# A transformer layer with a 16384-expert feed-forward: the gathered experts cut to 35 slots per token, their overflow listed per token half, and the last U blocks moved into the pipeline

## The chip, the cores and the metric

The kernel is written in Bass and Tile for one Trainium2 chip and runs on one of its cores. A core has TensorE (PE, matrix products into PSUM), VectorE (DVE), ScalarE (ACT), GpSimd (POOL) and SyncE (SP); each runs its own queue in order, and they wait for each other by semaphores. PE, DVE, ACT and POOL compute; SP and POOL issue DMAs here. The metric is the device time of one execution in microseconds (us). The profile is one execution recorded instruction by instruction.

## The reference, cut to what matters

The layer takes 256 tokens of width 2048 through a retention group and an RG-LRU group, a cross attention, and a feed-forward of 16384 single-neuron experts (PEER), then a final norm. Only the last is touched:

```python
def peer_ffn(xn, w_q, sub_keys, u_tab, v_tab):
    ...
    q = (xt @ w_q).reshape(t, PEER_HEADS, 2, PEER_HALF)
    sub_scores = jnp.einsum('thcd,hckd->thck', q, sub_keys).astype(jnp.float32)
    vals, ids = lax.top_k(sub_scores, PEER_TOPK)
    cand = vals[:, :, 0, :, None] + vals[:, :, 1, None, :]
    top_sc, pos = lax.top_k(cand.reshape(t, PEER_HEADS, PEER_TOPK * PEER_TOPK), PEER_TOPK)
    ...
    eid = (i1 * PEER_N_KEYS + i2).reshape(t, PEER_HEADS * PEER_TOPK)
    gate = jax.nn.softmax(top_sc, axis=-1).reshape(t, PEER_HEADS * PEER_TOPK)
    ...
        u = u_tab[eb]
        act = jax.nn.gelu(jnp.einsum('td,tkd->tk', xb, u).astype(jnp.float32))
        return jnp.einsum('tk,tkd->td', (gb * act).astype(xb.dtype), v_tab[eb])
```

Each token picks 128 experts (8 heads of 16). For each, the dot product of the token with the expert's row of `u_tab` goes through a gelu, is weighted by the gate, and scales the expert's row of `v_tab`, which is added to the token.

## The kernel before

**Two ways for the experts.** The table is cut by a row number, (i1 + i2) mod 128. Rows 0 to 95 (`RD`) are computed for all tokens as dense products: U gives the activations, the gates multiply them (zero where a token did not pick the expert), V gives the sum. Rows 96 to 127 are gathered: for each token the picked experts of these rows are fetched one by one. One gather (`rows`, L1132) brings one expert's row for each of the 128 tokens of a half, a megabyte, with an indirect DMA on POOL's queue. A token half has `BASE` = 36 slots, 72 in both; each slot costs a gather from `Us` with a `dot` (L1149, DVE) and a gather from `Vs` with an `axpy` (L1159, DVE).

**Overflow.** A token with more than 36 such experts puts the rest in two lists of 128 entries (`OV`) that both halves share. `compact` (L778) makes the slots and lists: picks by maxima on DVE, places by small matmuls on PE. `spill` (L1204) later fetches each list's U rows, its tokens' rows from `hn`, and its V rows (six gathers of a megabyte), takes the dots, and writes the weights as a one-hot matrix `oh`; sixteen matmuls (L971 to L974 or L994 to L998) add the V rows to their tokens in V chunk 9. If the lists do not hold everything, `rest` (L1226) runs a slow path under an `If`.

**Dense part.** Experts are in 12 chunks (`NCH`) of 8 blocks of 128. Each fp32 weight tile of 512 KB is loaded on SP, split by ACT (`hi`, a cast) and DVE (`lo`, the remainder), and multiplied in two parts. A U block takes two such tiles (halves) and 16 matmuls each; a V quarter takes one tile and 12.

**Order.** Up to the pipeline a planner orders the work, in the kernel's order as far as data allow: `u_chunk` (L928) does chunks 0 to 5 (`LEAD`), 96 halves. Beside them `Weave` feeds side work: after each half `pump` lets generators run for `wv.rate` credits, and each `yield` costs what it names. `RB` = 1.9 is the rate there. The side work is, in order, the rest of `route` (the top-16 searches, DVE), `gbuild` (L859) and `compact`. `gbuild` makes the dense gates: 64 groups of four tokens, each two comparisons on DVE, four scalings on ACT (L874), four matmuls `G` on PE (L884), and a copy on ACT (L886) into `gs`, which has two buffers; every fourth group one DMA on SP writes 768 KB to `gd` in DRAM. Chunk 5 has a stop: after its third block (L939 to L941) all that is left of `gbuild` is run, then `prep(0)` (L897) loads the gates of chunk 0, multiplies them on and splits the result.

From there `run` (L1079) issues by hand a list of steps, with up to 8 loads ahead: 6 times V chunk i (16 steps) and U chunk i + 6 (16 steps), woven with the `prep_steps` (L1041) of the next chunk; then V chunks 6 to 10 alone (80 steps). In all 272 steps with a weight tile. Within the list each engine's order is the order of the code. After each step `pump` at `RC` = 1.17 runs `chosen` (L1169), which does dots and axpys (2.2 credits each, and 0.225 per slot for the gates of a block, `weigh`, L1142), gathering three tasks ahead into four buffers (`ring`). What is left of it after the list is drained (L1360). Then come `rest` and `v_final` (L1247): V chunk 11, the last sums, the final norm and the output.

Of the kernel before, what the change touches and what calls it, by code (L numbers as in the profile page):

```python
# [32 lines left out]
RA, RB, RC = 1.1, 1.9, 1.17  # L33
# [38 lines left out]
def hybrid_layer_kernel(ctx: ExitStack, tc: tile.TileContext, a: dict, out: bass.AP, dbg=None):  # L72
# [705 lines left out]
    def compact():  # L778
        ct = pgt.tile([P, 7, TT], F32, tag="ct", name="ct")
        cnt, more, off, end, tok, off1, end1 = (ct[:, n] for n in range(7))  # L780
# [23 lines left out]
        V.tensor_scalar(fit, end, float(OV * P), None, op0=ALU.is_le)  # L804
# [14 lines left out]
        spl["t"] = tp.tile([P, OV], F32, tag="spt", name="spt")  # L819
        spl["ti"] = tp.tile([P, OV], I32, tag="spti", name="spti")  # L820
        spl["i"] = tp.tile([P, OV], I32, tag="spi", name="spi")
        spl["g"] = tp.tile([P, 40], F32, tag="spg", name="spg")[:, :OV]
# [633 lines left out]
```

## Time and profile before

| | us |
|---|---|
| three runs: lowest, median, highest | 2092.3, 2092.89, 2096.95 |
| the profiled execution, its own time | 2099.48 |
| its span, first to last instruction | 2097.7 |
| PE, DVE, ACT, POOL busy | 2030.7, 1698.7, 1039.0, 342.0 |
| loads of U tiles, V tiles (192 each), median to landing | 4.9, 7.9 |
| gathers from `Us`, `Vs` into `gat`, median to landing | 9.4, 9.6 |
| mean granted TensorE clock | 0.993 |

Busy time is the union of an engine's instructions. A matmul's end is modelled, so the pace of matmuls (how many in a stretch) says more than their busy time. The windows view gives, for stretches of the span in us, each engine's busy time and number of instructions, then the clock granted to PE, the busy share of the 16 DMA engines and the GB/s that they moved. In the timeline a row is: start, duration, engine, line, operation, output <- input, number, and in brackets the idle time before and what ended it.

### The profile page before, as it was taken

To read this page: it belongs to the slowest core of one execution; us is meant where nothing else is said; L and a number is where in the kernel's file an instruction comes from. 1 tells how busy PE (TensorE), PEld (TensorE's weight loads), DVE (VectorE), ACT (ScalarE), POOL (GpSimd) and SP (SyncE) were. 2 spreads that over 40 slices of the span, in tenths; PEclk is the share of its full clock that TensorE was granted. 3 is DMA by queue.
4 is the path that set the end of the run, shared out by engine and by line. 5 is a ranking of instruction groups with operands and counts; after the bars stand their busy time and mean duration, and the time that the engine had idled before them with its cause. 6 is when DMAs were issued, how large, how long until landed. Compare 5 with 4: busy or idle time off the path is not lost.

```text
span 2097.7 us, 29005 instructions
## 1 busy us (share of the span) xinstructions
PE 2030.7 (97%) x10452; PEld 1721.0 (82%) x10452; DVE 1698.7 (81%) x2455; ACT 1039.0 (50%) x1600; POOL 342.0 (16%) x195
## 2 busy tenths in 40 slices
PE   8999999999999999999999989999999999989997
PEld 6888878888888888888889968888888888767785
DVE  6859866744554457999987779999999999989897
ACT  6565434544544455554578853444444444433334
POOL 0200021000000000000000002323333332445342
PEclk9999999999999999999999999999999999999999
DMA  8675646566654468555686579999999999999874
GB/s 283 236 233 171 218 134 184 172 191 190 184 170 141 143 188 283 170 182 179 192 275 192 171 242 371 389 382 400 362 354 358 351 378 409 375 371 391 315 263 157
DMA packets 155015, 542.92 MB, mean 259 GB/s; under 512 B 17136, under 2 KB 44400, under 8 KB 136560
## 3 DMA queue, kind: packets, MB, share of 16 engines
q1 hardware_dynamic: 132832, 400.48, 56.7%
q0 software_dynamic: 22032, 140.53, 16.9%
q8 instruction: 82, 1.34, 0.3%
q14 instruction: 69, 0.57, 0.1%
HBM read 541.99 MB, written 18.87 MB: 267 GB/s over the span
## 4 chain that ended last, share of the span: by engine, by line
PE 77%; DVE 14%; DMA 4%; issue 3%; ACT 1%; POOL 1%; ACTq 0%; DVEq 0%; SPq 0%; POOLq 0%
PE U L129 13%; PE wb L129 8%; PE U L131 7%; PE xc L171 6%; PE xc L172 6%; PE xc L174 6%; PE acc L956 5%; PE acc L953 5%; PE acc L954 5%; PE wb L131 4%; DVE lo L120 4%; PE G L884 2%; PE V L956 2%; PE V L953 2%; PE V L954 2%
## 5 line engine op out<-in xcount | busy, mean ns | idle before, releaser
L120 DVE TENSOR_TENSOR lo<-raw,hi 128x1024 fp32r<-128x1024 f32 x396 | 486.0, 1230 | 261.9 <-PE xc L174 118.8
L119 ACT CAST hi<-raw 128x1024 fp32r<-128x1024 f32 x396 | 415.3, 1050 | 301.2 <-PE xc L172 165.2
L1092 ACT CAST hi<-raw 128x1024 fp32r<-128x1024 f32 x272 | 283.9, 1049 | 265.6 <-PE acc L954 91.1
L129 PE MATMUL U<-xn,hi 128*128 128x512 f32 x1536 | 401.7, 398 | 7.8 <-ACT hi L119 6.1
L1098 DVE TENSOR_TENSOR lo<-raw,hi 128x1024 fp32r<-128x1024 f32 x272 | 328.2, 1221 | 35.0 <-issue 16.6
L129 PEld LDWEIGHTS U<-xn,hi 128*128 128x128 f32 x1536 | 277.8, 190 | 58.3 <-ACT hi L119 6.2
L1135 POOL DMA_INDIRECT gat<-in_Us_dram,idx x69 | 122.2, 1771 | 682.6 <-DVE gat L1152 424.5
L131 PEld LDWEIGHTS U<-xn,lo 128*128 128x128 f32 x1536 | 210.1, 190 | 18.3 <-DVE lo L120 2.3
L131 PE MATMUL U<-xn,lo 128*128 128x256 f32 x1536 | 218.5, 284 | 1.8 <-DVE lo L120 1.3
L1152 DVE SCALAR_TENSOR_TENSOR gat<-gat,h 128x2048 f32<-128x2048 f32 x69 | 157.7, 2285 | 0.0
L953 PE MATMUL acc<-hi,ah 128*128 128x512 f32 x384 | 150.7, 392 | 1.5 <-DVE foldu L937 1.5
L954 PE MATMUL acc<-hi,al 128*128 128x512 f32 x384 | 150.4, 392 | 0.0
L129 PE MATMUL wb<-hT,hi 128*128 128x512 f32 x448 | 119.8, 400 | 0.0
L956 PE MATMUL acc<-lo,ah 128*128 128x512 f32 x384 | 103.4, 391 | 4.9 <-DVE lo L120 3.4
L1135 POOL DMA_INDIRECT gat<-in_Vs_dram,idx x39 | 86.7, 2223 | 130.3 <-DVE hh L1160 112.7
L129 PE MATMUL wb<-xT,hi 128*128 128x512 f32 x368 | 93.4, 394 | 2.1 <-ACT hi L119 2.1
L129 PEld LDWEIGHTS wb<-hT,hi 128*128 128x128 f32 x448 | 81.3, 189 | 14.0
L1160 DVE SCALAR_TENSOR_TENSOR hh<-gat,coef,hh 128x2048 f32<-128x2048 f32 x39 | 91.5, 2346 | 0.1
L956 PEld LDWEIGHTS acc<-lo,ah 128*128 128x128 f32 x384 | 71.9, 188 | 21.8 <-DVE lo L120 4.7
L1135 POOL DMA_INDIRECT h<-in_Vs_dram,idx x33 | 70.7, 2144 | 108.3 <-DVE hh L1160 101.5
L953 PEld LDWEIGHTS acc<-hi,ah 128*128 128x128 f32 x384 | 72.5, 189 | 16.8 <-DVE foldu L937 1.8
L954 PEld LDWEIGHTS acc<-hi,al 128*128 128x128 f32 x384 | 72.6, 189 | 15.2
(411 smaller groups left out, 3654.4 us busy)
## 6 DMA issues: line engine op xcount, KB each, us to landing
raw<-in_U_dram SPq DMA_DIRECT2D x192, 512.0 KB, 4.9
raw<-in_V_dram SPq DMA_DIRECT2D x192, 512.0 KB, 7.9
raw<-in_w_xyg_dram SPq DMA_DIRECT2D x48, 512.0 KB, 4.5
raw<-in_w_qkv_dram SPq DMA_DIRECT2D x48, 512.0 KB, 4.2
raw<-in_w_xk_dram SPq DMA_DIRECT2D x32, 512.0 KB, 3.6
raw<-in_w_xv_dram SPq DMA_DIRECT2D x32, 512.0 KB, 4.2
raw<-in_w_out_dram SPq DMA_DIRECT2D x32, 512.0 KB, 4.2
raw<-in_w_xq_dram SPq DMA_DIRECT2D x32, 512.0 KB, 3.5
```

Of the source, the lines that this page charges most:

```text
L119: A.copy(hi, raw)
L120: V.tensor_tensor(lo, raw, hi.bitcast(F32), op=ALU.subtract)
L129: PE.matmul(pt, hi[:, ks], xt[:, kb, :], start=(kb == 0), stop=(kb == KB - 1))
L131: PE.matmul(pt[:, :T], lo[:, ks], xt[:, kb, :T], start=False, stop=False)
L171: PE.matmul(pt, xh, hi[:, w], start=(n == 0 and k == 0), stop=False)
L953: PE.matmul(pt, ah[:, c, t_], hi[:, w], start=(first and c == 0), stop=False)
L954: PE.matmul(pt, al[:, c, t_], hi[:, w], start=False, stop=False)
L956: PE.matmul(pt, ah[:, c, t_], lo[:, w], start=False, stop=(last and c == 7))
L1092: A.copy(his[t], raws[t])
L1098: V.tensor_tensor(los[t], raws[t], his[t].bitcast(F32), op=ALU.subtract)
L1135: G.indirect_dma_start(gat, None, a[tab], bass.IndirectOffsetOnAxis(ap=idx[tt][:, k:k + 1], axis=0), bounds_check=NS - 1, oob_is_err=False)
L1152: V.scalar_tensor_tensor(gat, gat, 1.0, h[0], op0=ALU.mult, op1=ALU.mult, accum_out=dots[tt, k0][:, k:k + 1])
```

## The change

Seven edits go together. The slots are 35 per token half (70, from 72). The overflow has one list of 128 for each half, with its own tokens only, so the places need one matmul and each list one matmul per kind of column. `compact` takes turns with `gbuild`, yield by yield, and ends with filling the gather buffers (three zero fills, on POOL; they were on DVE). In `gbuild` every second copy is DVE's, and the write to `gd` is issued on POOL. `RB` is 2.35. Chunk 5 does two blocks (`CUT`) in `u_chunk`; its other six are 12 steps at the head of the list, woven with the `prep_steps` of chunk 0, and the stop for `gbuild` is gone; `hh` is loaded at step 8. `spill` is gone: `chosen` ends with the six gathers, two dots, and the weights, and the list's V rows are added by eight matmuls as the last row operations of V chunk 11, in `v_final`. The warm-up of ACT's square root in `v_final` now reads `oh`.

```diff
-RA, RB, RC = 1.1, 1.9, 1.17
+RA, RB, RC = 1.1, 2.35, 1.17
...
-BASE = 36
+BASE = 35
...
-OV = 2
 LEAD = 6
+CUT = 2
...
     def compact():
...
-        PE.matmul(pt[:, 0:1], tri[:, :P], cnt[:, 0:1], start=True, stop=True)
-        PE.matmul(pt[:, 1:2], ones, cnt[:, 0:1], start=True, stop=False)
-        PE.matmul(pt[:, 1:2], tri[:, :P], cnt[:, 1:2], start=False, stop=True)
+        PE.matmul(pt[:, :TT], tri[:, :P], cnt, start=True, stop=True)
...
-        own = rp.tile([P, TT, OV * P], F32, tag="eq", name="own")
...
-        for tt in range(TT):
-            for b, (first, last) in enumerate(((off, end), (off1, end1))):
-                cut = tp.tile([P, P], F32, tag="gj", name="cut")
-                ts, os = slice(tt, tt + 1), slice(b * P, (b + 1) * P)
-                V.tensor_scalar(own[:, tt, os], iota, first[:, ts], fit[:, ts], op0=ALU.is_ge, op1=ALU.mult)
-                V.tensor_scalar(cut, iota, last[:, ts], fit[:, ts], op0=ALU.is_ge, op1=ALU.mult)
-                V.tensor_tensor(own[:, tt, os], own[:, tt, os], cut, op=ALU.subtract)
+        own = rp.tile([P, TT, P], F32, tag="eq", name="own")
+        yield 0.8
+        for tt in range(TT):
+            cut = tp.tile([P, P], F32, tag="gj", name="cut")
+            ts = slice(tt, tt + 1)
+            V.tensor_scalar(own[:, tt], iota, off[:, ts], fit[:, ts], op0=ALU.is_ge, op1=ALU.mult)
+            V.tensor_scalar(cut, iota, end[:, ts], fit[:, ts], op0=ALU.is_ge, op1=ALU.mult)
+            V.tensor_tensor(own[:, tt], own[:, tt], cut, op=ALU.subtract)
             yield 0.8
...
+        for b in range(TT):
+            bs = slice(b, b + 1)
             pt = sm("spill")
             for n, cols in enumerate((lambda tt: sel[tt][:, BASE:], lambda tt: gsp[tt],
...
-                for tt in range(TT):
-                    PE.matmul(pt[:, c0:c1], own[:, tt, os], cols(tt), start=(tt == 0), stop=(tt == TT - 1))
+                PE.matmul(pt[:, c0:c1], own[:, b], cols(b), start=True, stop=True)
             yield 1.5
...
             yield 0.6
...
-    side = []
+        ring.extend(slot("ms", [P, D], f"gat{n}") for n in range(3))
+        for gat in ring:
+            G.memset(gat, 0.0)
+        ring.append(h[1])
+
+    def turns(one, two):
+        for x in one:
+            yield x
+            y = next(two, None)
+            if y is not None:
+                yield y
+        yield from two
+
+    ring = []
...
                 for j in range(4):
                     PE.matmul(pt[:, j * RD:(j + 1) * RD], o1[:, j, :], o2[:, j, :RD], start=True, stop=True)
                 g0 = 4 * (m % 4)
-                A.copy(gs[:, :, g0:g0 + 4, :],
-                       pt[:, :4 * RD].rearrange("p (t c x) -> p c t x", t=4, x=8))
+                (V.tensor_copy if m % 2 else A.copy)(
+                    gs[:, :, g0:g0 + 4, :], pt[:, :4 * RD].rearrange("p (t c x) -> p c t x", t=4, x=8))
                 if m % 4 == 3:
                     tl = slice(4 * m - 12, 4 * m + 4)
-                    nc.sync.dma_start(gd[:, :, tl, :].rearrange("q p t c -> p q t c"), gs)
+                    G.dma_start(gd[:, :, tl, :].rearrange("q p t c -> p q t c"), gs)
                 yield 0.4
...
-    def prep(i):
...
-    def u_chunk(i):
+    ahs, spare = {}, {}
...
-        for c in range(8):
+        for c in blocks:
...
             for j in range(0 if i or c else 1, 2):
                 whalf(j, a["U"][8 * i + c, j], xn, pt)
-                tick(2 * c + j)
...
             A.activation(act[:, c, :], t, AF.Gelu_apprx_tanh)
-            if i == LEAD - 1 and c == 2:
-                while "gbuild" not in done:
-                    wv.pump(3.0)
-                wave.append(prep(0))
-        flush()
...
-        late = i == SPILL + 2
+        late = i == NCH - 1
...
         if late:
             for tt in range(TT):
-                for b in range(OV):
-                    PE.matmul(pts[tt], spl["oh"][:, b, tt * P:(tt + 1) * P],
-                              spl["v"][b][:, dc * 512:(dc + 1) * 512], start=False, stop=(last and b == OV - 1))
+                PE.matmul(pts[tt], spl["oh"][:, tt], spl["v"][tt][:, dc * 512:(dc + 1) * 512],
+                          start=False, stop=last)
...
-                late = i == SPILL + 2
-                v_mms(ah, al, hi, lo, q, list(enumerate(box)), not kept or i == 0, not kept and not late)
-                if late and q == 3:
-                    for tt in range(TT):
-                        for b in range(OV):
-                            PE.matmul(box[tt], spl["oh"][:, b, tt * P:(tt + 1) * P],
-                                      spl["v"][b][:, dc * 512:(dc + 1) * 512], start=False,
-                                      stop=(not kept and b == OV - 1))
+                v_mms(ah, al, hi, lo, q, list(enumerate(box)), not kept or i == 0, not kept)
 
...
         for t, step in enumerate(steps):
+            if t == 8:
+                for tt in range(TT):
+                    nc.sync.dma_start(hh[tt], hd[tt])
...
-    def chosen(blocks):
...
+        dots_left = sum(t[0] is dot for t in tasks)
+        extra = [lambda: fetch(next_gat(), a["Us"], NS, spl["i"][:, 0:1]),
+                 lambda: spill_x(1, next_gat()),
+                 lambda: fetch(next_gat(), a["Us"], NS, spl["i"][:, 1:2])] if tail else []
         for m in range(len(tasks) + AHEAD):
             if m < len(tasks):
                 f, tab, tt, k0, n, k = tasks[m]
                 held.append(rows(tab, tt, k0 + k))
+            elif extra:
+                held.append(extra.pop(0)())
...
                 if f is dot and not any(t[0] is dot and t[2] == tt for t in tasks[m - AHEAD + 1:]):
                     hold(min([t[2] for t in tasks[m - AHEAD + 1:] if t[0] is dot], default=tt))
+                    if tail and not dots_left:
+                        spill_x(0, h[0])
                 yield 2.2
+        if tail:
+            spill_dot(0, held[-3], h[0])
+            spl["v"] = [next_gat() for b in range(TT)]
+            yield 2.2
+            spill_dot(1, held[-1], held[-2])
+            yield 2.2
+            spill_rows()
+            spill_weights()
...
-    def spill():
-        od = cp.tile([P, OV], F32, name="od")
-        for b in range(OV):
-            bs = slice(b, b + 1)
-            u, x = fetch("Us", spl["i"][:, bs], "ah"), fetch(None, spl["ti"][:, bs], "al")
-            yield
-            yield
-            V.scalar_tensor_tensor(u, u, 1.0, x, op0=ALU.mult, op1=ALU.mult, accum_out=od[:, bs])
-            yield
-        spl["v"] = [fetch("Vs", spl["i"][:, b:b + 1], ("ah", "al")[b]) for b in range(OV)]
+    def fetch(dst, src, n, ix):
+        G.indirect_dma_start(dst, None, src, bass.IndirectOffsetOnAxis(ap=ix, axis=0),
+                             bounds_check=n - 1, oob_is_err=False)
+        return dst
+
+    def next_gat():
+        turn[0] += 1
+        return ring[(turn[0] - 1) % len(ring)]
+
+    def spill_x(b, dst):
+        if b == 0:
+            kept_h[0] = None
+        return fetch(dst, hn, T, spl["ti"][:, b:b + 1])
+
+    def spill_dot(b, u, x):
+        if b == 0:
+            spl["d"] = cp.tile([P, TT], F32, name="od")
+        V.scalar_tensor_tensor(u, u, 1.0, x, op0=ALU.mult, op1=ALU.mult, accum_out=spl["d"][:, b:b + 1])
...
+    def spill_weights():
+        od = spl["d"]
...
+        spl["oh"] = rp.tile([P, TT, P], F32, tag="eq", name="oh")
+        for b in range(TT):
+            bs = slice(b, b + 1)
+            V.tensor_scalar(spl["oh"][:, b], iota, spl["t"][:, bs], od[:, bs], op0=ALU.is_equal, op1=ALU.mult)
+
+    def spill_rows():
+        for b in range(TT):
+            fetch(spl["v"][b], a["Vs"], NS, spl["i"][:, b:b + 1])
...
+            spill_rows()
...
-        A.activation(warm, iota[:, 0:1], AF.Sqrt)
+        A.activation(warm, spl["oh"][:, 0, 0:1], AF.Sqrt, scale=0.0)
...
             pt = mm("V0")
             for q in range(4):
-                v_mms(ah, al, vl[:, q, 0], vl[:, q, 1], q, [(tt, pt)])
+                v_mms(ah, al, vl[:, q, 0], vl[:, q, 1], q, [(tt, pt)], last=False)
+            PE.matmul(pt, spl["oh"][:, tt], spl["v"][tt][:, ds], start=False, stop=True)
...
-    wv.add(gbuild())
-    wv.add(compact())
+    wv.add(turns(gbuild(), compact()))
     wv.rate = RB
     for i in range(LEAD):
-        u_chunk(i)
+        u_chunk(i, range(8 if i < LEAD - 1 else CUT))
+    wv.drain()
     hh = [slot("qs", [P, D], f"hh{tt}") for tt in range(TT)]
-    for tt in range(TT):
-        nc.sync.dma_start(hh[tt], hd[tt])
-    wv.drain()
...
-    ring = [slot("ms", [P, D], f"gat{n}") for n in range(3)] + [h[1]]
-    for gat in ring[:3]:
-        V.memset(gat, 0.0)
...
-    wv.add(chosen(blocks_of(0, 0, BASE) + blocks_of(1, 0, BASE)))
-    steps = []
+    wv.add(chosen(blocks_of(0, 0, BASE) + blocks_of(1, 0, BASE), True))
+    steps = woven(list(u_steps(LEAD - 1))[2 * CUT:], prep_steps(0), 6, 3)
     for i in range(NCH - 1):
         if i + LEAD < NCH:
             steps += woven(v_steps(i), [], 0, 0)
             steps += woven(u_steps(i + LEAD), prep_steps(i + 1), 3, 4)
         else:
             steps += woven(v_steps(i), prep_steps(i + 1), 2, 4)
-        if i == SPILL - 1:
-            mark = len(steps)
...
```

More of the change, by code (lines that the diff above doesn't have):

```diff
@@ L778, in compact @@
     def compact():
-        ct = pgt.tile([P, 7, TT], F32, tag="ct", name="ct")
-        cnt, more, off, end, tok, off1, end1 = (ct[:, n] for n in range(7))
+        ct = pgt.tile([P, 5, TT], F32, tag="ct", name="ct")
+        cnt, more, off, end, tok = (ct[:, n] for n in range(5))
         tri = rp.tile([P, P + 1], F32, tag="cand", name="tri")
@@ L803, in compact @@
         V.tensor_tensor(end, off, cnt, op=ALU.add)
-        V.tensor_scalar(fit, end, float(OV * P), None, op0=ALU.is_le)
+        V.tensor_scalar(fit, end, float(P), None, op0=ALU.is_le)
         V.tensor_tensor(cnt, fit, more, op=ALU.mult)
@@ L807, in compact @@
         V.tensor_scalar(flag, fit, -1.0, 1.0, op0=ALU.mult, op1=ALU.add)
-        own = rp.tile([P, TT, OV * P], F32, tag="eq", name="own")
-        V.tensor_scalar(off1, off, -float(P), None, op0=ALU.add)
-        V.tensor_scalar(end1, end, -float(P), None, op0=ALU.add)
+        own = rp.tile([P, TT, P], F32, tag="eq", name="own")
+        yield 0.8
         for tt in range(TT):
-            for b, (first, last) in enumerate(((off, end), (off1, end1))):
-                cut = tp.tile([P, P], F32, tag="gj", name="cut")
-                ts, os = slice(tt, tt + 1), slice(b * P, (b + 1) * P)
-                V.tensor_scalar(own[:, tt, os], iota, first[:, ts], fit[:, ts], op0=ALU.is_ge, op1=ALU.mult)
-                V.tensor_scalar(cut, iota, last[:, ts], fit[:, ts], op0=ALU.is_ge, op1=ALU.mult)
-                V.tensor_tensor(own[:, tt, os], own[:, tt, os], cut, op=ALU.subtract)
-            yield 0.8
[L819 to L822, printed above, removed]
-        for b in range(OV):
-            bs, os = slice(b, b + 1), slice(b * P, (b + 1) * P)
+            cut = tp.tile([P, P], F32, tag="gj", name="cut")
[3 more added lines that the diff above has]
+            V.tensor_tensor(own[:, tt], own[:, tt], cut, op=ALU.subtract)
+            yield 0.8
+        spl["t"] = tp.tile([P, TT], F32, tag="spt", name="spt")
+        spl["ti"] = tp.tile([P, TT], I32, tag="spti", name="spti")
+        spl["i"] = tp.tile([P, TT], I32, tag="spi", name="spi")
+        spl["g"] = tp.tile([P, 64], F32, tag="spg", name="spg")[:, :TT]
+        for b in range(TT):
+            bs = slice(b, b + 1)
             pt = sm("spill")
@@ L836, in compact @@
             V.tensor_copy(spl["ti"][:, bs], spl["t"][:, bs])
+            if b:
+                V.tensor_scalar(spl["t"][:, bs], spl["t"][:, bs], -float(b * P), None, op0=ALU.add)
             w1 = pgt.tile([P, 3], F32, tag="w1", name="w1")
-            V.tensor_scalar(w1[:, 0:1], ls[:, OVK + P + 1:], -1.0, float(b * P), op0=ALU.mult, op1=ALU.add)
+            V.tensor_scalar(w1[:, 0:1], ls[:, OVK + P + 1:], -1.0, None, op0=ALU.mult)
             V.tensor_tensor(w1[:, 0:1], w1[:, 0:1], tri[:, P:], op=ALU.add)
@@ L1028, in curved @@
         def curved(c):
-            if c == 0:
+            if i not in acts:
                 acts[i] = tp.tile([P, 8, T], F32, tag="act", name=f"act{i}", bufs=LEAD)
@@ L1167, in hold, with chosen @@
             G.dma_start(h[0], hn[tt * P:(tt + 1) * P, :])
-    def chosen(blocks):
+    def chosen(blocks, tail=False):
         tasks = []
@@ L1215, in spill @@
         V.tensor_tensor(od, od, spl["g"], op=ALU.mult)
-        spl["oh"] = rp.tile([P, OV, T], F32, tag="eq", name="oh")
-        for b in range(OV):
-            for tt in range(TT):
-                bs = slice(b, b + 1)
-                V.tensor_scalar(spl["oh"][:, b, tt * P:(tt + 1) * P], iota, spl["t"][:, bs], od[:, bs],
-                                op0=ALU.is_equal, op1=ALU.mult)
-                V.tensor_scalar(spl["t"][:, bs], spl["t"][:, bs], -float(P), None, op0=ALU.add)
-        yield
@@ L1224, in spill @@
-        done.add("spill")
+        spl["oh"] = rp.tile([P, TT, P], F32, tag="eq", name="oh")
[5 more added lines that the diff above has]
+            fetch(spl["v"][b], a["Vs"], NS, spl["i"][:, b:b + 1])
     def rest():
@@ L1348, in hybrid_layer_kernel @@
             steps += woven(v_steps(i), prep_steps(i + 1), 2, 4)
-        if i == SPILL - 1:
-            mark = len(steps)
-    def begin(f):
-        def g(*x):
-            side.append(spill())
-            f(*x)
-        return g
-    steps[mark] = steps[mark][:2] + (begin(steps[mark][2]),) + steps[mark][3:]
     with tc.manual_schedule(engines=ENGINES):
```

45 lines of the change are left out of this document (2 added, 43 removed).

## The prediction, made before the changed kernel was run

> **What bounds the kernel now.** I read the page first, then busy time by stretches (the windows view), then the timeline at the seams.
>
> ```profile
> span 2097.7 us, 29005 instructions
> PE 2030.7 (97%) x10452; PEld 1721.0 (82%) x10452; DVE 1698.7 (81%) x2455; ACT 1039.0 (50%) x1600; POOL 342.0 (16%) x195
> ```
>
> PE is busy 97% of the span, but those are unions of modelled matmuls; what counts is where they fall below their pace. The stretches from the first U block on (PE, PEld, DVE, ACT, POOL, then granted clock, DMA share, GB/s):
>
> ```profile
> 910.00:1040.00 130.00, 130.00 (x744) 113.91 (x744) 130.00 (x357) 67.09 (x105) 0.00 (x0) 1.00 0.61 185
> 1080.00:1180.00 100.00, 100.00 (x677) 91.60 (x677) 73.50 (x110) 85.67 (x227) 0.00 (x0) 1.00 0.69 204
> 1180.00:1217.00 37.00, 36.02 (x265) 33.47 (x264) 27.81 (x46) 34.93 (x113) 0.00 (x0) 1.00 0.40 125
> 1217.00:1247.00 30.00, 22.00 (x120) 19.14 (x119) 21.05 (x59) 13.57 (x23) 0.00 (x0) 0.83 0.84 299
> 1247.00:1780.00 533.00, 529.42 (x2673) 449.75 (x2674) 514.16 (x533) 236.50 (x305) 170.93 (x97) 1.00 0.96 371
> 1780.00:1840.00 60.00, 57.39 (x253) 46.29 (x253) 59.75 (x62) 22.99 (x24) 28.27 (x12) 1.00 0.97 380
> 1840.00:1870.00 30.00, 23.73 (x97) 17.34 (x95) 20.65 (x18) 11.22 (x11) 8.04 (x5) 1.00 0.98 401
> 1870.00:1960.00 90.00, 81.68 (x336) 63.62 (x337) 88.23 (x90) 32.20 (x34) 46.44 (x19) 0.98 0.95 370
> 1960.00:2000.00 40.00, 40.00 (x156) 29.14 (x155) 32.44 (x34) 12.77 (x14) 10.88 (x7) 1.00 0.80 285
> 2000.00:2038.00 38.00, 38.00 (x169) 31.45 (x169) 37.21 (x30) 16.47 (x18) 19.45 (x7) 1.00 0.78 270
> 2038.00:2060.00 22.00, 18.59 (x74) 14.16 (x73) 21.75 (x16) 5.60 (x6) 6.95 (x3) 0.92 0.54 178
> ```
>
> Three stages lie here. **U stage, to 1247:** PE at its pace, with DVE full beside it until 1040 (`route`), and a hole at 1217 to 1247, where PE works 22 of 30 us at a clock of 0.83. **Mixed steps, 1247 to 1780:** 192 steps, PE 529 of 533 us and DVE 514: both are full, PE decides. **V chunks 6 to 10, 1780 to 2038:** DVE is busy 59.75 + 20.65 + 88.23 + 32.44 + 37.21 = 238.3 of 258 us and PE less, except in 1960 to 2000, where PE is full and DVE is not. So here DVE decides, with 19.7 us of holes, which come from a DMA stall (1840 to 1870, DMA share 0.98) and from PE. What each unit of work costs PE, from the windows of U and of G alone:
>
> ```profile
> 910.00:1040.00 130.00, 129.92 (x741) 1.00 0.61 185
> 1080.00:1180.00 100.00, 74.65 (x395) 1.00 0.69 204
> 1080.00:1180.00 100.00, 34.58 (x282) 1.00 0.69 204
> ```
>
> A U half is 16 matmul records: 130 / (741 / 16) = 2.81 us. A gate group is 8 records (the third row): 395 records are 24.7 halves or 69.4 us, which leaves 30.6 us for 35 groups, 0.87 us each.
>
> **The U stage.** It begins and ends here:
>
> ```profile
> 895.82 1.55 PE L129 MATMUL U<-xn,hi 128*128 128x512 f32 x6
> ...
> 1213.19 1.26 PE L884 MATMUL G<-o,o 128*128 128x96 f32 x8 [0.18 <-ACT o L874]
> 1214.68 1.26 PE L884 MATMUL G<-o,o 128*128 128x96 f32 x8 [0.22 <-ACT o L874]
> ...
> 1233.93 3.70 PE L129 MATMUL U<-xn,hi 128*128 128x512 f32 x8 [6.08 <-ACT hi L119]
> ...
> 1246.57 0.39 PE L129 MATMUL U<-xn,hi 128*128 128x512 f32 x1
> ```
>
> 96 halves at 2.81, 64 groups at 0.87 and some 5 us of list matmuls make 330.5 us; from 895.8 to 1246.9 it takes 351, so 20.6 are lost. Most of that is at the stop in chunk 5: the groups left run at ACT's pace (1214.68 - 1213.19 = 1.49 us), then the lists, then a wait of 6.08 us for the cast behind all that. The stop goes away. In its place stand 84 halves (236.0), 55.7 for the groups and 3 for half the list matmuls: 294.7. To this I add what stays lost.
>
> ```profile
> 1040.00:1050.00 10.00, 9.08 (x52) 7.61 (x50) 9.63 (x20) 5.15 (x8) 0.00 (x0) 1.00 0.51 166
> 1050.00:1060.00 10.00, 8.72 (x50) 7.58 (x51) 9.18 (x16) 3.66 (x6) 2.38 (x2) 1.00 0.85 325
> ...
> L120 DVE TENSOR_TENSOR lo<-raw,hi 128x1024 fp32r<-128x1024 f32 x46 | 55.5, 1206 | 0.0
> L937 DVE TENSOR_TENSOR foldu<-U,foldu 128x256 f32<-128x256 f32 x23 | 9.5, 411 | 0.0
> ...
> gat<-in_Us_dram,idx POOLq DMA_INDIRECT x69, 9.4
> raw<-gd SPq DMA_DIRECT2D x24, 512.0 KB, 8.1
> ```
>
> (a) `route` at the new rate. In 910 to 1040 DVE had no idle time at 1.9 credits a half; at 2.35 the 102 credits of `route` meet 44 halves, not 54. Ten halves fewer take 10 x 1.4 us (a `lo` and half a fold) off DVE and 28 off PE, so up to 14 us of DVE lag appear; before, the end of `route` (1040 to 1060) cost PE 2.2. I take 5 (bounds 0 and 14). The three fills that leave DVE (1.76 us each, row below) help here. (b) Credits: 83 pumps x 2.35 = 195, against 102 for `route`, 83 for `gbuild`, 17 for `compact` and a rest of `normed`: about nine groups are left for the drain, 9 x (1.49 - 0.87) = 5. (c) 2.5 for the first step behind the drain, a cast and a `lo`. Then 12 steps at 2.81 = 33.7, with ACT and DVE below their load in the mixed steps. (d) The first gathers now stand on POOL behind the last `gd` write, so DVE, in order, may wait in its first dot, with every later `lo` behind it. Against that stand four `lo`, eight `weigh` and PE's stored steps, four times 2.81 = 11 us of cover, and a landing of 9.4: I take 2 (0 to 8). Sum 294.7 + 12.5 + 33.7 + 2 = 343 against 351: **8 us gained** (bounds -8 and 18). The gates' load at step 9 needs the last `gd` write; it has the work of eight steps (22 us) ahead of it, against 5.3 us landing of the write (row below) and 8.1 of the load: nothing.
>
> The copies moved to DVE, 32 of them, cost there about what they cost ACT (0.47 us, first row below); DVE was busy 73.5 of 100 us in 1080 to 1180, so they are hidden, and ACT (85.7) is relieved. The DMA that moves to POOL is not shown there; the nearest rows:
>
> ```profile
> L886 ACT COPY gs<-G 128x384 f32<-128x384 f32 x64 | 29.8, 471 | 3.3 <-PE G L884 3.0
> ...
> L673 POOL DMA_DIRECT2D hn<-h x2: 572/660/749, 814.6 to 817.2; - x2
> L1135 POOL DMA_INDIRECT gat<-in_Us_dram,idx x69: 984/1732/7632, 1050.2 to 2004.2; - x69
> gd<-gs SPq DMA_DIRECT2D x16, 768.0 KB, 5.3
> 1059.53 1.76 DVE L1336 MEMSET gat<- 128x2048 f32 x1 [0.37 <-issue]
> ```
>
> A direct write of 128 rows took POOL 0.66 us, a gather of 128 rows 0.98 to 7.63. A `gd` write has 12 pieces per row: between 0.66 us (a fixed price) and 12 x 1.73 = 20.8 us (by the piece, as the median gather). Four groups take about 4 x (0.87 + 2.81 / 1.8) = 9.7 us, at 2.35 / 1.3 = 1.8 groups a half. Below that POOL, idle in this stretch, hides it; I take 12 x 0.66 = 7.9, the nearest row by the piece, at no cost, and keep the rest as a rival. The fills stand on POOL too, 1.76 us each there as on DVE, up to four times that by POOL's slowest row; no write is due in the 10 us behind them, and they cost nothing.
>
> [...]
>
> **V chunks 6 to 10.** What fills DVE's holes:
>
> ```profile
> 1834.74 7.63 POOL L1135 DMA_INDIRECT gat<-in_Us_dram,idx  x1 [0.30 <-issue]
> ...
> L1098 DVE TENSOR_TENSOR lo<-raw,hi 128x1024 fp32r<-128x1024 f32 x80 | 96.0, 1226 | 17.6 <-ACT hi L1092 10.3 <-issue 5.7 <-PE acc L956 1.5
> ...
> 1962.73 3.59 PE L996 MATMUL V<-spl,oh 128*128 128x512 f32 x8
> ...
> L1211 DVE SCALAR_TENSOR_TENSOR spl<-spl 128x2048 f32<-128x2048 f32 x2 | 4.6, 2292 | 0.0
> L1220 DVE TENSOR_SCALAR oh<-iota,spt,od 128x128 f32<-128x128 f32 x4 | 1.6, 404 | 0.1
> ```
>
> `spill` puts two more megabytes on POOL at 1830, beside gathers already due; the weight tiles come late and DVE waits 10.3 us behind ACT. Its 32 records in chunk 9 (8 per column block, 3.59 us, 0.43 a piece) make PE the bound for 13.8 us, and DVE idles 7.6. Both go: the six gathers now take turns with the tasks, and the matmuls leave. Credits per step stay at 1.17, so DVE's load per step stays; 1.1 us go with two of the four `oh` operations. Of 19.7 + 1.1 I take **17** (bounds 5 and 21), for the second dot has its gather only two tasks ahead, about 11 us, against a landing of 9.4 and more in a full stretch.
>
> **The end.** Before, 6.7 tasks were left for the drain (72 slots x 4.625 credits = 333 against 272 x 1.17 = 318), and DVE kept PE waiting:
>
> ```profile
> 2055.55 1.21 PE L956 MATMUL acc<-lo,ah 128*128 128x512 f32 x4 [2.20 <-DVE lo L120]
> ...
> 2087.69 0.61 PE L956 MATMUL V<-vl,ah 128*128 128x512 f32 x2
> ```
>
> From 2038.4 to 2088.3 PE takes 49.9 us for 16 quarters (12 records at 0.227, 2.72 each: 43.5): 6.4 lost. Now 70 x 4.625 + 4.4 = 328 credits meet 284 x 1.17 = 332: the work ends three steps before the list does, and the loss goes. In come eight matmuls, 16 records at 0.43 = 6.9, on the path. **Nothing gained** (-3 to 3). The lists' V rows are fetched some 7 steps (19 us) before their first matmul; nothing. The mixed steps keep their work: nothing. The single edits of `compact` and the warm-up lie beside PE's work: nothing.
>
> **Sum.** 8 + 17 + 0 = 25 us: a span near 2073. The profiled execution took 2099.48, 6.6 over the median of 2092.89; taken from the median, **2068**. The bounds of the terms added in quadrature reach from 2057 to 2088; without what stands below as rivals, this case spans 2057 to 2079.
>
> **The rivals.** (1) *The U stage gains nothing:* DVE stays `route`'s bound at 2.35 and the first dot waits, its term near -3: 2079. For: DVE 130.00 of 130. Against: PE stood at its pace there too. (2) *DMA takes DVE's place in chunks 6 to 10.* A step needs 0.52 MB of weights, 0.53 of gathers and 0.07 of gates; 80 steps and six gathers are 96 MB, at the 401 GB/s of 1840 to 1870 239 us, just DVE's 238, at 371 as in the mixed steps 259: no gain there, 2085; half of it, 2077. [...] (3) *Slower: POOL cannot keep up with the `gd` writes.* `gs` has two buffers, so past 9.7 us a write the copies wait, and with them the casts of U on ACT. 16 writes at p cost 16 x (p - 9.7): the gain is eaten at p = 11.3; at 20.8 it is 178 us against the 25, about 2245. Against: fixed parts do not grow by the piece. (4) *The lists overflow:* 116 and 78 entries of 128, counted from the reference's own routing, so the slow path stays shut; taken, 2 x 93 slots more, 372 operations of 2.29, past 2900. (5) *More is gained*, both terms at their upper bounds: 2052.
>
> **Chances.** Forecast 0.50; (1) 0.17; (2) 0.15; (3) 0.08; (4) 0.01; (5) 0.06; (1) with (2), 2087 to 2096, 0.03. For 8 in 10 the range takes in (1), most of (2) and part of (5): 2050 to 2086. A measurement of this kernel tells about 0.2%, 4 us, from no change. Faster by more: the forecast, (1), (5), nearly all of (2), half of (3)'s milder end, 0.86; within it 0.05; slower 0.09.
>
> **What would show it.** Right: no stretch without U matmuls between 900 and 1200, PE waiting under 3 us at the seam; no DVE idle beside a DMA share near 1 in the last V chunks; none of its time lost to a drained tail. Wrong: POOL busy with `gd` writes of 10 us or more, ACT waiting for `gs`; a first dot that waits long; the steps of chunks 6 to 10 still near 3.2 us.

## The result and the profile after

The changed kernel takes 2083.95 us (median of 6 runs, 2079.47 to 2085.61) against 2094.28 for the kernel before (2090.22 to 2098.95): a ratio of 0.9947, 95% interval 0.9933 to 0.9962. It is faster, by 0.5%; 2068 was forecast. Here is the head of the page of after:

```profile
span 2083.4 us, 28880 instructions
...
PE 2022.8 (97%) x10416; PEld 1717.1 (82%) x10416; DVE 1694.3 (81%) x2461; ACT 1031.2 (49%) x1570; POOL 375.4 (18%) x210
```

The shares of busy time tell nothing: 97% as before. The stages do. From PE's timeline of both executions I read the start of the first U matmul, the start of the first V matmul, and the ends of the last mixed step and of chunk 10; the stages lie between them (us):

| stage | before | after | gained | forecast |
|---|---|---|---|---|
| U stage | 353.2 | 359.2 | -6 | 8 |
| mixed steps | 534.3 | 542.3 | -8 | 0 |
| V chunks 6 to 10 | 255.7 | 228.3 | 27 | 17 |
| the end, with what follows PE | 59.2 | 60.7 | -1.5 | 0 |

With 2.3 ahead of the first U block this makes the 14 us between the two spans. The medians differ by 10.3 only: the trace of before is of an execution 5.2 us above its median, that of after 1.4, so some 4 us of the table belong to that one execution, in a stage that is not known. Both large terms of the forecast were off, in opposite directions. Stretches of after (PE, PEld, DVE, ACT, POOL, granted clock, DMA share, GB/s), then the same of before:

```profile
892.00:1080.00 188.00, 177.22 (x1020) 154.26 (x1019) 181.70 (x501) 98.77 (x179) 11.85 (x9) 0.98 0.60 191
1200.00:1300.00 100.00, 84.47 (x415) 71.01 (x414) 81.44 (x110) 42.26 (x76) 23.44 (x15) 0.91 0.84 313
1300.00:1790.00 490.00, 489.57 (x2498) 416.96 (x2497) 476.49 (x483) 220.88 (x287) 170.47 (x90) 1.00 0.98 381
1794.50:2022.70 228.20, 222.07 (x962) 178.80 (x961) 224.13 (x197) 95.94 (x99) 111.10 (x40) 1.00 0.95 358
```

```profile
892.00:1080.00 188.00, 183.66 (x1067) 161.14 (x1066) 185.99 (x497) 102.50 (x176) 4.36 (x4) 1.00 0.64 206
1200.00:1300.00 100.00, 89.59 (x473) 76.90 (x472) 80.88 (x150) 49.81 (x98) 13.11 (x8) 0.95 0.81 295
1782.80:2038.50 255.70, 238.50 (x995) 185.80 (x994) 236.11 (x221) 95.74 (x98) 112.48 (x47) 0.99 0.91 347
```

The mixed steps themselves (1300 to 1790) run at PE's pace; what they lost lies at their start. PE is short in two places: under `route`, where it lost 10.8 of 188 us instead of 4.3, and at the seam between the gates' building and the listed steps, 1200 to 1300, where the old stop went (10.4 us of holes at a clock of 0.95) and 15.5 us of holes at 0.91 came in its place. In chunks 6 to 10 DVE has 4.1 us of holes, not 19.6, and also 12.0 us less to do.

The holes of the seam, in PE's timeline of after (start, length, in brackets the idle time and what ended it):

```profile
1220.55 3.78 PE L129 MATMUL U<-xn,hi 128*128 128x512 f32 x8 [3.99 <-DVE foldu L982]
...
1229.80 2.14 PE L129 MATMUL U<-xn,hi 128*128 128x512 f32 x8 [0.77 <-ACT hi L1048]
...
1239.29 3.18 PE L129 MATMUL U<-xn,hi 128*128 128x512 f32 x8 [3.43 <-ACT hi L1048]
...
1255.11 0.50 PE L925 MATMUL acc<-hi,al 128*128 128x512 f32 x1 [2.58 <-DVE al L1020]
...
1265.60 0.80 PE L925 MATMUL acc<-hi,al 128*128 128x512 f32 x1 [4.76 <-DVE al L1020]
```

Each wait is for ACT or DVE, but these are only in between: a `lo`, a fold or an `al` stands on DVE behind a `lo` that waits for a cast, and the cast waits for a weight tile (ACT's casts waited 30.6 us for weights between 1210 and 1310). The first of them are late because their queue stood still. SP's waits in 1180 to 1240 (total, times, longest):

```profile
SPq L1043 <- PE G L892: 28.8, 2, 28.3
SPq L1043 <- DMA gd<-gs: 14.0, 1, 14.0
```

First SP waits 28.3 us for the room of two weight tiles, in which the gates' tiles still lie; then 14.0 us for the last `gd` write, which the second gates' load needs. Every weight load stands behind. What was missed then comes at once: the seven V tiles issued from 1237 to 1254 took 9.6 to 18.3 us to land, the four U tiles issued from 1171 to 1184 3.4 to 5.2. Why that write is late is seen on DVE, then on POOL:

```profile
1214.34 2.29 DVE L1111 SCALAR_TENSOR_TENSOR gat<-gat,h 128x2048 f32<-128x2048 f32 x1
...
1216.55 0.55 DVE L894 COPY gs<-G 128x384 f32<-128x384 f32 x1
```

```profile
1216.90 1.06 POOL L1094 DMA_INDIRECT gat<-in_Us_dram,idx  x1 [7.07 <-DVE gat L1111]
1217.97 1.06 POOL L898 DMA_DIRECT2D gd<-gs  x1
```

The last copy is on DVE behind the first dot, and the write on POOL behind a gather that waits for the same dot. And `gd`'s answer in the trace:

```profile
L898 POOL DMA_DIRECT2D gd<-gs x16: 1018/1021/1093, 1051.5 to 1218.0; - x16
...
DMA to landing us min/median/max: 4.9/5.3/13.1
```

A write holds POOL for 1.02 to 1.09 us, with 12 pieces per row, so rival 3 did not occur. But the longest landing, that of the last write, is 13.1 us.

### The profile page after: what moved, and what is told of

The parts are those of the page before. It is cut to its first block, busy times and chain, and to the rows that moved or that the text cites. A ratio compares the mean times of both kernels' runs of the same rounds, so it can differ in the third digit from the quotient of the medians.

```text
span 2083.4 us, 28880 instructions
## 1 busy us (share of the span) xinstructions
PE 2022.8 (97%) x10416; PEld 1717.1 (82%) x10416; DVE 1694.3 (81%) x2461; ACT 1031.2 (49%) x1570; POOL 375.4 (18%) x210
## 4 chain that ended last, share of the span: by engine, by line
PE 80%; DVE 12%; DMA 5%; issue 2%; ACT 1%; POOL 0%; SPq 0%; ACTq 0%; DVEq 0%; POOLq 0%
PE U L129 14%; PE U L131 7%; PE wb L129 7%; PE xc L171 6%; PE xc L172 6%; PE xc L174 6%; PE acc L927 6%; PE acc L925 5%; PE acc L924 5%; PE wb L131 4%; DVE lo L120 3%; PE G L892 2%; PE V L927 2%; DMA raw<-in_V_dram 2%; PE V L924 2%
## 5 line engine op out<-in xcount | busy, mean ns | idle before, releaser
L1111 DVE SCALAR_TENSOR_TENSOR gat<-gat,h 128x2048 f32<-128x2048 f32 x65 | 148.5, 2285 | 0.0
L1094 POOL DMA_INDIRECT gat<-in_Vs_dram,idx x40 | 81.5, 2038 | 125.8 <-DVE hh L1119 115.9
L1094 POOL DMA_INDIRECT h<-in_Vs_dram,idx x30 | 81.3, 2709 | 102.4 <-DVE hh L1119 94.6
```

The costliest lines, as they stand in the source:

```text
L1094: G.indirect_dma_start(gat, None, a[tab], bass.IndirectOffsetOnAxis(ap=idx[tt][:, k:k + 1], axis=0), bounds_check=NS - 1, oob_is_err=False)
L1111: V.scalar_tensor_tensor(gat, gat, 1.0, h[0], op0=ALU.mult, op1=ALU.mult, accum_out=dots[tt, k0][:, k:k + 1])
```

## The experiments

To compare the seam, I take the time from the first U matmul to DVE's first gates multiplication of chunk 1, which stands at the same step in all kernels: 401 us before, 415 after, 393 by the forecast. Kernels with the same seam (after, its repeat x13, x6) gave 415, 415 and 409, so that under 6 us a single trace decides nothing. Medians are of 4 to 12 runs.

**x13, the changed kernel again**, beside x14 to x16.

> The changed kernel once more, beside the versions below on one chip. If the chips agree, 2082 to 2086 us, and what is read off against it is read rightly.

2085.0 us (ratio 0.9953, 0.9933 to 0.9973): the chips agree.

**x1, two rates.**

```
-RA, RB, RC = 1.1, 2.35, 1.17
+RA, RB, RC, RB2 = 1.1, 1.9, 1.17, 3.0
         done.add("route")
+        wv.rate = RB2
```

> The changed kernel, but with 1.9 credits a half while the routing lists are made (as before the change), and 3.0 from the end of `route` on, so that the gates are built by about the same time. If the higher rate during `route` is what PE paid for early in the U stage (10.8 us short of full between 895 and 1080, where DVE is full), PE is short there by 2 to 4 us, and the kernel takes about 2077 us. Rival: 3.0 credits overload DVE or ACT while the gates are built, and the same time is lost between 1080 and 1200: 2084. If the whole loss is at the seam, no change either.

2082.05 us (0.9934 to 0.9972). Under `route` PE is back at its old pace:

```profile
892.00:1080.00 188.00, 184.43 (x1067) 161.93 (x1067) 184.12 (x490) 100.75 (x172) 11.50 (x8) 0.99 0.65 208
```

So the rate cost 7.2 us there. The seam, which begins with the first U matmul and so includes this stretch, took 409; and this execution (2087.07 us, 5 above the median) lost 9 us in chunks 6 to 10. There one gather held POOL for 13 us, and the second list's dot waited for the gather behind it (POOL's, then DVE's timeline):

```profile
1985.82 13.07 POOL L1175 DMA_INDIRECT gat<-hn,spti  x1 [1.71 <-DVE hh L1120]
```

```profile
2011.59 2.29 DVE L1191 SCALAR_TENSOR_TENSOR gat<-gat,gat 128x2048 f32<-128x2048 f32 x1 [6.75 <-DMA gat<-in_Us_dram,spi]
```

**x2 to x4: four tiles; all of chunk 5; `hh` apart.**

```
x2:  -  raws[t] = spot[t % 6]
     +  raws[t] = spot[t % 4 if t < 12 else (t - 12) % 6]
x3:  -CUT = 2
     +CUT = 0
     -  prep_steps(0), 6, 3)
     +  prep_steps(0), 10, 3)
x4:  -  if t == 8: (both halves of hh)
     +  if t in (8, 15): (one half each)
```

In x2 the loads go six steps ahead up to step 12, not eight, and steps 9 and 10 work on values of later loads.

> The changed kernel, but the first twelve loads of the pipeline turn among four weight tiles and leave the two tiles alone that stand in the gates' room, so that SP does not stop 28.3 us for that room. Theory A (weight loads stand on SP behind stopped issues: the room of the gates first, then the gates' load that waits 14.0 us for the last `gd` write): the first of the two stops goes, PE's wait of 4.0 us at 1216 with it, and the second stays: 2079 to 2081 us. Theory B (the seam is short of DMA throughput: 2 MB of `hh` beside gathers, gates and weights): no change, 2084.

> The changed kernel, but all 16 halves of U's chunk 5 go into the pipeline, not 12, and the gates of chunk 0 are loaded four steps later. Theory A: the second gates' load reaches SP's head some 11 us later against the last `gd` write, its wait falls from 14 us to 0 to 4, and PE's waits behind it (0.8, 3.4, 2.6 and 4.8 us, and the low clock after them) mostly go: 2073 to 2077 us. Theory B: the same bytes in the same stretch, 2082 to 2086.

> The changed kernel, but the second half of `hh` (1 MB) is loaded at step 15 of the pipeline, not with the first at step 8. Theory B: 1 MB less in the stretch 1235 to 1255, 2.5 us of DMA at 419 GB/s, and the weights of the first V steps come that much earlier: 2079 to 2081 us. Theory A: the SP queue's stops are over by then, and what was lost stays lost: 2083 to 2085.

2088.2, 2088.8 and 2082.7 us. Nothing was gained. In x2 SP waited for tiles instead of room, and PE stopped once for 12 us. In x3 the wait for the write was gone, but SP stood 42 us for the room, and the seam took 418. x4's 412 is within the spread. Neither theory holds as it stands.

**x5, the two tiles in another room, and x9, that with all of chunk 5.**

```
+  first = tp.tile([P, 8, T], F32, tag="al", name="first")...   # two tiles of 1024
-  raws[t] = spot[t % 6]
+  raws[t] = first[t % 6 - 4] if t < 12 and t % 6 > 3 else spot[t % 6]
```

> The changed kernel, but the pipeline's first twelve steps put their fifth and sixth weight tile into the room of `al`, which is free then, and not into the gates' room; the tiles, the distance and all else stay. Theory C (SP stops for the gates' room, 28.3 us here and 42 us with all of chunk 5 in the pipeline; the DMA queues run dry, and what they missed must then come at 419 GB/s with `hh`, the gates and the first gathers): the stop goes, weights for the first eight halves are there when the last `gd` write lands, PE's 4.0 us wait at 1216 goes and the later ones (0.8, 3.4, 2.6 and 4.8) shrink by half or more: 2074 to 2079 us. Rival D (the wait for the last `gd` write alone makes the backlog): SP stands still for it all the same, 2082 to 2085.

> The two tiles in `al`'s room and all 16 halves of U's chunk 5 in the pipeline, with the gates of chunk 0 loaded four steps later. Each alone left one of SP's two stops (28.7 us for the last `gd` write, or 42 us for the room), and each alone gained nothing. Theory F (one stop is as long as the other, both end with the last gates at about 1215 to 1225, and either makes the same backlog): with both gone PE waits under 5 us in all between 1200 and 1290, and the U stage and the mixed steps together fall from 901 to about 888: 2070 to 2075 us. Theory B (bytes alone): the stretch stays at 415 GB/s and PE still loses 12 us or more: 2082 to 2088.

2086.1 and 2088.8 us; seam 412 and 416. Theory C falls with x5: the room's stop was gone, and SP stood 28.7 us for the write, in three waits. Theory F falls with x9, whose SP met neither stop for long; among its waits in 1160 to 1260 were

```profile
SPq L1044 <- DVE lo L1055: 56.6, 11, 14.2
...
SPq L1044 <- DMA gd<-gs: 7.0, 1, 7.0
```

and PE lost 6.40 us to a cast all the same, at 1250. The cast waited 10.8 us for its weight tile, with DMA at a share of 1.01 (418 GB/s) in 1235 to 1250. Something else had to be short as well.

**x11, no wait for gates, and x12, a slow start.** In x11 the loads of chunk 0's gates read rows of V.

```
x11 (on x5):  +  src = gd[i, ...] if i else a["V"][0, tt, 0]
x12:  -  wv.pump(wv.rate)                          # in the pipeline, RC = 1.17
      +  wv.pump(0.5 if t < 16 else wv.rate)       # RC = 1.21
```

> The two tiles in `al`'s room, and chunk 0 is multiplied by rows of V in place of its gates (its gates are left out of the result), so that the loads have the same size and place and wait for no `gd` write. Theory F: SP stops for nothing, PE waits under 5 us in all between 1200 and 1290: 2070 to 2075 us. Theory B: the bytes are the same, 2082 to 2086.

> The changed kernel, but with 0.5 credits a step in the pipeline's first 16 steps and 1.21 behind them: some four gathers (4 MB, 10 us of DMA at 419 GB/s) fewer in the stretch 1220 to 1290. Theory B: the weights come through, PE's waits behind 1235 go, 6 to 10 us gained, less 2 to 3 for DVE's fuller chunks 6 to 10: 2076 to 2081. Theory F: the SP stops are unchanged, the lead is rebuilt sooner behind them, 2 to 3 us gained and given back: 2082 to 2086.

2080.2 us against x5's 2086.1, and 2087.9. Their seams took 406 and 405, each well below after's 415. The stretch 1200 to 1300 of x11, then of x12:

```profile
1200.00:1300.00 100.00, 93.57 (x473) 78.86 (x472) 91.84 (x121) 46.27 (x84) 26.76 (x17) 0.95 0.87 334
```

```profile
1200.00:1300.00 100.00, 90.66 (x477) 77.67 (x477) 82.86 (x114) 45.71 (x80) 20.35 (x13) 0.98 0.85 320
```

So there are two causes, the wait for the write and the first row operations: up to the seam's end x12 issues 10 gathers, after 14. Each gather left out spares a megabyte of DMA and, once it has landed, 2.3 us of DVE for its dot, so x12 alone does not tell which of the two counts (x18 does, below). x12 gained 10 us at the seam and lost 11 in chunks 6 to 10 (239.3 us), where its row operations now came.

**x6, the lists as before, and x7, credits earlier.** Two runs on the gain of chunks 6 to 10.

```
x6:  +  side.append(spill())      # at chunk 7's first step: fetches and dots outside the credits
     +  if i == 9 and q == 3:     # the list matmuls, out of v_unit and v_final
x7:  -RC = 1.17
     +RC = 1.20
     +  if t == 218:
     +      wv.rate = 1.08
```

> The changed kernel, but the two lists' rows are fetched and multiplied in chunk 7 and 8 outside the credits, their matmuls are in chunk 9, as before the change. If the even gathers and the matmuls' place gave the gain in chunks 6 to 10 (27 us, of which some 15 were holes in DVE's work), half of it or more goes back, and the end gets 16 records or 6.9 us shorter: 2088 to 2094 us. If most of the gain there is that DVE has less to do in these chunks (fewer row operations are left for them), it stays: 2078 to 2084.

> The changed kernel, but with 1.20 credits a step up to the last mixed step and 1.08 behind it, so that some seven credits, three row operations, move from chunks 6 to 10 into the mixed steps. If DVE decides in chunks 6 to 10 (224.6 busy of 228.7 us there) and has room in the mixed steps (490.5 of 504): 5 to 8 us gained, 2076 to 2079. Rivals: DMA decides in chunks 6 to 10, and nothing is gained there; or DVE is full in the mixed steps already, and what is gained is lost there: 2083 to 2086 either way.

2085.4 and 2080.3 us. Chunks 6 to 10 of x6, then of x7:

```profile
1787.90:2027.50 239.60, 229.97 (x978) 183.32 (x978) 225.06 (x197) 98.73 (x101) 102.36 (x40) 0.99 0.90 342
```

```profile
1797.60:2020.50 222.90, 219.99 (x962) 179.31 (x960) 217.32 (x191) 96.62 (x100) 81.85 (x37) 1.00 0.94 354
```

The old form of the lists costs 11.3 us here (239.6 against 228.3), of which 10.5 are holes of DVE, but x6's end is 7.1 us shorter: the form is worth 4 net. The other 16 us of the 27 stay: 11 are work that DVE no longer has there (225.1 us, not 236.1), 5 are fewer holes than before even so (14.5, not 19.6), whose cause no run shows. x7 takes 6.8 us more off DVE and gains 5.4: DVE decides there.

**x8 and x10, edits added up** (x8: x5, x1 and x4; x10: those with x3 and x7).

> The two tiles in `al`'s room, the two rates (1.9, then 3.0 from the end of `route`) and the second half of `hh` at step 15, together. If the losses add up: 7 from the rates, 5 to 9 from the room, 1 to 2 from `hh`, 2067 to 2072 us. If the seam's loss is set by the last `gd` write whatever comes ahead of it: about 2075 to 2080.

> x9 with the two rates, the second half of `hh` at step 15, and 1.20 credits a step up to the last mixed step, 1.08 behind it. By theory F the gains add up: 12 at the seam, 7 in `route`'s stretch, 5 in chunks 6 to 10: 2058 to 2066 us. By theory B only 5 of the credits and some of the rates: 2074 to 2080.

2082.6 and 2075.7 us; seams 407 and 408. x10 is ahead by x7's credits. The gains at the seam did not add up.

**x14, all copies on ACT; x15 and x16, without and with them.**

```
x14:  -  (V.tensor_copy if m % 2 else A.copy)(gs...
      +  A.copy(gs...
x15 (on x8):  +  wv.pump(0.5 if t < 16 else wv.rate if t < 218 else 1.13)       # RC = 1.20
x16:  x15 with x14's edit
```

> The changed kernel with all copies of the gates on ACT, as before the change. The last copy is then not behind the first dot on DVE, and no gather stands ahead of a `gd` write on POOL. If the lateness of the last write (dot, copy, gather, write: 1214.3 to 1218.0) is what makes the seam's loss, the write goes out 2 to 4 us sooner, before the gathers load the DMA queues, and lands in 5 us, not 13: 6 to 10 us gained, 2074 to 2078. If ACT becomes the bound while the gates are built (97.8 of 120 us there, and 32 copies of 0.47 more), or the bytes decide at the seam: 2082 to 2088.

> The two tiles in `al`'s room, the two rates, the second half of `hh` at step 15, and credits of 0.5 a step in the first 16 steps, 1.20 up to the last mixed step and 1.13 behind it; the copies stay split. x12 gained 10 us at the seam and gave them back in chunks 6 to 10, where the credits came late; here most of them come in the mixed steps. If the gains add up (10 at the seam, 6 in `route`'s stretch, 1 to 2 more in chunks 6 to 10): 2064 to 2070 us. If the mixed steps cannot take 1.20, or the seam is short for another reason: 2074 to 2080.

> x15 with all copies of the gates on ACT. If the late last write still costs at the seam of x15: 3 to 6 us less than x15. If not, the same within 2 us; if ACT becomes the bound at 3.0 credits a half: 5 to 10 us more than x15.

2082.9, 2077.0 and 2070.0 us; seams 412, 397 and 391. POOL's last write in x14, x15 and x16:

```profile
1218.21 1.03 POOL L898 DMA_DIRECT2D gd<-gs  x1 [5.89 <-ACT gs L894]
```

```profile
1218.39 1.03 POOL L899 DMA_DIRECT2D gd<-gs  x1 [6.96 <-ACT foldu L979]
```

```profile
1206.73 1.03 POOL L899 DMA_DIRECT2D gd<-gs  x1 [4.70 <-ACT gs L895]
```

What helps is not where the copies stand but when the last write leaves. In x14 it went as late as in after, and nothing was gained. In x15 it was as late too; the seam was 18 us better than after's by the two rates (7) and the slow start. In x16 ACT finishes the gates at once, ahead of nearly all of the pipeline's steps; the write leaves 12 us sooner. SP's waits for the write in 1180 to 1240, in x15 and then in x16:

```profile
SPq L1045 <- DMA gd<-gs: 40.6, 3, 23.5
```

```profile
SPq L1045 <- DMA gd<-gs: 4.9, 1, 4.9
```

In x15 DVE waited 8.7 us for the gates themselves. In x16 PE has hardly a hole at the seam:

```profile
1200.00:1300.00 100.00, 98.34 (x501) 83.14 (x501) 90.79 (x112) 49.34 (x74) 23.77 (x14) 1.00 0.91 346
```

Its U stage takes 343.7 us; by the ends of the table above the forecast for the change was 345 (353.2 less 8).

**x17 and x18, what x16 needs.** x17 leaves out the room and the split of `hh` and has 1.17 for 1.13; x18 leaves out the slow start (credits as in x7).

> x16 without the room in `al` and with both halves of `hh` at step 8, as in the changed kernel, and with 1.17 credits a step in chunks 6 to 10, not 1.13, since x16's last list matmuls waited for the list (its end took 57.3 us, not 50.9). Left are the two rates, the copies on ACT and the slow start. If the early last write and the few first gathers are what matters at the seam, its time from the first U block to the gates of chunk 1 stays within 3 us of x16's 391; the end comes back to 51 at 2 to 3 us more in chunks 6 to 10: 2065 to 2069 us. If SP's stop for the gates' room counts once the other waits are gone: 4 to 8 us more at the seam, 2070 to 2075.

> x16 without the slow start: 1.20 credits a step from the first step on, 1.08 in chunks 6 to 10. The write is as early as in x16, the gathers as many as in the changed kernel. If the bytes of the first gathers cost by themselves (x12: 10 us), the seam loses 6 to 10 us against x16, and chunks 6 to 10 and the end gain 2 and 6: 2070 to 2074 us. If they cost only behind a late write, the seam stays as in x16: 2061 to 2066.

2067.3 us (ratio to before 0.9882, 0.9865 to 0.9898; with x16, 0.9869 to 0.9903, the fastest here) and 2072.6. x17's seam takes 393 although SP stands nearly as long as in after for the room:

```profile
SPq L1044 <- PE G L893: 26.9, 1, 26.9
```

So that stop cost no more than the 2 us between x16 and x17, within the spread, once the write was early. x18's seam takes 401, 10 more than x16's: the first row operations cost 10 us behind an early write as behind a late one (x12). Here that is DVE, not bytes. The same stretch of x18, then of x16:

```profile
1212.00:1248.60 36.60, 30.60 (x159) 25.14 (x158) 36.60 (x37) 15.46 (x24) 14.84 (x6) 0.93 0.95 364
```

```profile
1212.00:1248.60 36.60, 36.41 (x193) 30.92 (x192) 33.50 (x32) 19.60 (x27) 6.24 (x3) 1.00 0.95 370
```

The DMA share is 0.95 in both, and x18 moves no more than x16. But DVE has no idle time in x18: it does seven dots where x16 does four, and PE waits for what stands behind them, 1.78 us for a fold at 1217 and, at 1245, for an `al`:

```profile
1245.01 0.79 PE L926 MATMUL acc<-hi,al 128*128 128x512 f32 x1 [3.49 <-DVE al L1021]
```

So behind an early write it is DVE that the first dots overload. Behind a late write the weights are short as well (the landings of 9.6 to 18.3 us in after; the cast of x9), and how much of x12's 10 us is bytes there stays open.

## Why the prediction was half right

**The U stage, forecast 8 gained, lost 6, and 8 more in the first mixed steps.** This is the step that failed, in three terms. That 2083.95 us still lies between the stated 2050 and 2086 is luck: chunks 6 to 10 gave 10 us more than forecast and hid part of it.

*The gates' load.* "It has the work of eight steps (22 us) ahead of it [...]: nothing." The gates themselves were hardly waited for (0.20 and 0.69 us on DVE). But a load that is issued eight steps ahead also reaches its wait eight steps ahead, and SP issued nothing past it (the next weight load left at 1231.74, behind the 14.0 us): the cover that I counted for the load was what the load behind it lost. The write landed in 13.1 us, not 5.3. I asked this question of each queue that a DMA was moved past, and not of the queue that now held the waiting load. An early write is worth 6 us at the seam and 7 in the median (x15 against x16; the copies themselves, moved in x14 alone, gained nothing); x11 puts the wait at 5 and 6 (against x5).

*The row operations at the start.* "Then 12 steps at 2.81 = 33.7, with ACT and DVE below their load in the mixed steps" puts them at nothing. But these steps have the mixed steps' share of `lo` and folds, credits from the first step on, and the two gates multiplications besides: by the rows of after some 37 us of DVE (12 `lo` of 1.22, 6 folds of 0.42, 14 credits of row operations and `weigh` with 15.5, twice 2.1), an estimate, against PE's 33.7. In x18 DVE is full there, 36.60 of 36.60 us. In after, behind the late write, DMA is short beside it: 2 MB of `hh`, the gates and up to the seam's end 14 gathers, not 8 as before, come with the weights that SP held back, at 419 GB/s in 1240 to 1260. Four gathers and their dots fewer are worth 10 us (after against x12, x18 against x16). Rival 2, "DMA takes DVE's place", is a part of this, at the seam and not in chunks 6 to 10; how large a part no run shows.

*`route` at the new rate.* Forecast 5, with 14 as the bound; 10.8 were lost, 7.2 of which x1 wins back. The mechanism was right and the size too small.

Term (d), the first dot's gather behind the last write, was the other way round: the first four gathers left at 1050.0 to 1055.6, and the write stood behind the fifth. The prediction's own row shows the first gather at 1050.2 in before.

Beyond what the forecast had charged, these are 6 us (the write), 10 (the row operations) and 6 (`route`, 10.8 less 5), 22 in all, which is what U stage and mixed steps missed. That they agree so well is chance, for they are differences of single traces under a spread of some 6 us. x16, which has all three remedies, takes 882.2 us for both stages together, 19 less than after.

**V chunks 6 to 10, forecast 17, measured 27, above the bound of 21.** The mechanism was right: DVE decides, and its holes fell by 15.5 us. (As the trace of before lies above its median, 27 may be too much by up to 4.) The step "DVE's load per step stays" was wrong. The lists' two dots, 4.6 us, had stood outside the credits and now take their place in them; and the work ends before the credits do, which the prediction used for the end but not here. DVE had 20 dots and 22 axpys there before, and has 15 and 23 after, four row operations or 9 of the 12.0 us fewer:

```profile
L1152 DVE SCALAR_TENSOR_TENSOR gat<-gat,h 128x2048 f32<-128x2048 f32 x20 | 45.8, 2291 | 0.0
```

```profile
L1111 DVE SCALAR_TENSOR_TENSOR gat<-gat,h 128x2048 f32<-128x2048 f32 x15 | 34.3, 2285 | 0.0
```

**The end**, forecast 0, lost 1.1 up to the last matmul (50.9 us, not 49.8), within the bounds of 3. Rivals 3 and 4 did not occur. Rival 1 came closest for the U stage: its first reason, `route`, cost 6 us more than charged, its second, a first dot that waits, did not occur, and it was too mild.

## What to carry to other kernels

A DMA that is prefetched far ahead waits far ahead, too (here 14.0 us on SP): when a load with a late producer joins an in-order queue, cost the wait at the place where the queue reaches it, and count the loads behind it. Where DVE and DMA are near full in steady state (476.5 of 490 us and 0.98 here), a start that has work of its own needs slack, for instance fewer row operations in the first steps; and as a slow start relieves both, read from the trace which of them was short. And where work runs by credits, draw up its ledger over all stages: what is moved into the credits, or ends early, changes the load of the stage that is bound.

## What the runs showed of the hardware

Behind long PE waits the matmuls were slow as well. Eight U matmuls without a wait before them took 2.09 us (at 892.95 in after). Behind 3.99 us they took 3.78, behind 0.77 us 2.14 (rows of after above); behind 5.25, 6.16, 6.40 and 8.09 us (x5, x3, x9, x15) it was 3.78 again. Behind waits in between it varied: 2.11 behind 2.12 us in x5 and behind 2.76 in x13, 2.51 behind 2.54 in x14, 3.18 behind 3.43 in after. Four `sub` matmuls (L678; 0.61 us without a wait, at 895.83 in after) took 1.16 us behind 2.15 in after, but 0.71 behind 2.16 in x16:

```profile
898.59 1.16 PE L678 MATMUL sub<-kq,qp 128*128 128x128 f32 x4 [2.15 <-DVE qp L154]
```

```profile
898.95 0.71 PE L678 MATMUL sub<-kq,qp 128*128 128x128 f32 x4 [2.16 <-DVE qp L154]
```

So in these rows the length of the wait alone does not tell the pace behind it. The granted clock was low in the stretches with the long waits: 0.84 in 1220 to 1240 of after and 0.74 in the same of x15, against 1.00 in 1300 to 1790 of after. What sets it no run shows.

The time that a gather held POOL was 0.98 to 7.63 us in the trace of before and 0.99 to 8.74 in that of after, and reached 13.07 in x1; that of a `gd` write was 1.02 to 1.09. In after the writes were taken while DVE was busy 140.5 of 166.5 us (1051.5 to 1218), the gather of 8.74 us, at 1810, while it was busy 198.2 of 200 (1800 to 2000). No run here took the gathers away from DVE's work, so the cause stays open.
